# Attention by pairs of heads in a two-model fp32 kernel: scores on TensorE's row halves, values in plain fp32 on its column halves

## The chip, the cores and the metric

The kernel runs on one core of a Trainium2 chip, in one launch. The metric is device time in microseconds (us), the median over several runs. The kernel before takes 2503.48 us (three runs, 2503.0 to 2504.59). Times of single instructions come from one profiled execution and are given in us or ns.

## What is computed

Two small models run one after the other on 256 tokens of width 1024, all in fp32. Each has two layers. The first mixes a convolution, a neighbourhood attention ("na"), a dilated attention ("dil") and a windowed attention with a sink ("swa"), each of the three with 4 heads of 64 dims; the second mixes a Fourier branch, a convolution and a latent attention with 8 heads, over a stream x and, in its first layer, a context stream as well. Every attention comes down to this, for each head:

```python
s = jnp.einsum("bqhd,bkhd->bhqk", q, k) * scale + bias     # 256 x 256 scores of a head
p = jax.nn.softmax(s, axis=-1)
o = jnp.einsum("bhqk,bkhd->bqhd", p, v)                    # 64 dims of values
```

In the second model x looks at x and context (512 keys) and the context at itself (256 keys). The rest of the reference is projections, feed-forward blocks and norms, and these hold nearly all of the work.

## The kernel before

**Products in three parts.** TensorE gets its operands as `float32r`, a reduced fp32 that passes through the array once. To keep fp32's precision each operand is split into a high part and a low part: `parts` (L297 to L299) has ScalarE copy the source into a `float32r` tile and VectorE subtract it from the source. `mm3` (L301 to L305) then makes a product as high x high, high x low and low x high. L303, L304 and L305 are therefore the lines of nearly all matmuls of the profile.

**Weights** stream in from HBM, up to 512 KB a piece, are split by `parts` and used once. Activations stand with dims on the partitions and tokens along the free axis; a product of 256 tokens streams 256 columns, one of both streams together 512.

**Attention of the first model** (`attend1`, L826) is a generator for one head with three stages. Scores: two query tiles of 128, three matmuls each, with 64 rows of the array (`rows` is the upper or lower half, by the head's parity `e`), then bias, maximum, exponential and division on VectorE and ScalarE. Transpose: four 128 x 128 transposes of the probabilities into one PSUM bank (`tp`), then `parts` into PT. Values: `mm3` of V's 128 columns (both heads of the pair, of which one head's 64 are wanted) with PT, for two key tiles, into `py`; the head's 64 rows of `py` go through `parts` into `yt`, and `yt` is what the branch's products read.

**Order of the work.** `mix1` has 12 heads as a pipeline over slots: in a slot head k makes its scores, head k-1 its transposes, head k-2 its values, and after each of the three `more()` (L671) takes a unit from `fill` (projections of gates, of the convolution's input, and the branches' products, whose units read `yt`) and a few taps of the convolution on VectorE. A unit of gates is 24 matmuls of 256 columns. The order in which the instructions of an engine stand in the program is made by the build from this, with some moved between neighbours.

**Attention of the second model** (`attend2`, L1419) is the same for one head of one stream, with `mix2`'s slots around it: scores with all 128 rows, in a PSUM bank for each query tile; transposes, 8 for a head of x, 4 for one of the context; `parts` into PT; `mm3` for four or two key tiles of V, of 128 columns of which 64 are wanted.

In names such as `natp`, `diltp` and `hdtp` the first letters are the phase (na, dil, swa, hd for the second model's heads) and `tp` the PSUM tile, for the transposes and the values alike; `nasc`, `dilsc` and `swasc` are scores, `nar` is PT, `qkvV` and `vr` are V, `trr` and `hdr4b` are the values' results, `g1ps` a gates' product, `b1ps` a branch's, `ident` the identity of a transpose, `ones` a 128 x 128 tile of 1/1024 for sums over partitions. Those sums (L325, L326, L789 and others) are the only plain fp32 matmuls of the kernel; every other one is `float32r` or a transpose.

Of the kernel before, what the change touches and what calls it, by code (L numbers as in the profile page):

```python
# [17 lines left out]
P = 128  # L18
# [12 lines left out]
# ---------------------------------------------------------------- layout on the host  # L31
# [40 lines left out]
def host_arrays(inp):  # L72
# [10 lines left out]
    # [layer, chunk, quarter, 128, 2 row tiles, 512]  # L83
# [76 lines left out]
    # neighbourhood: bias of each pair inside the window, no weight outside  # L160
# [7 lines left out]
    # dilated: in how many of the three groups a key is seen  # L168
# [4 lines left out]
    # as a bias: the logarithm of the count  # L173
# [19 lines left out]
    # the queries' table has the scores' scale in it  # L193
# [15 lines left out]
# ---------------------------------------------------------------- the program  # L209


class Net:
# [13 lines left out]
    # -- tiles  # L226
# [42 lines left out]
    # -- weights  # L269
# [6 lines left out]
    def weights(self, src, raw=None):  # L276
        """High and low parts of a [128, a, b] piece of weights."""
# [29 lines left out]
    # -- rms norm over the partitions of several tiles; gives -2 / sqrt(mean + eps) on every partition  # L307
# [21 lines left out]
    def rsqrt(self, ps, w, f=1.0):  # L329
        """-2 / f / sqrt(f * ps + eps): f as the sums are over 1/1024, not the mean."""  # L330
# [14 lines left out]
    # -- constants  # L345
    def setup(self):
# [12 lines left out]
        # gains carry the -1/2 that norm_fin leaves  # L359
# [34 lines left out]
    def setup_later(self):  # L394
        """What the first model's first products don't need."""
# [28 lines left out]
    def ctx_root(self):  # L424
        """The root of the second stream's first norm."""
# [23 lines left out]
    # -- modulation: silu(c) @ w_mod, each column's sum along the free axis  # L449
# [7 lines left out]
    def mod_step(self, n, upto=(LAYERS,)):  # L457
        """The next n sums, before (layer, step, column), behind the weights split last."""
# [12 lines left out]
    def mod_in(self, l, step):  # L471
        """Per stream: factor on the normed x and shift of a step."""
# [14 lines left out]
    def mod_out(self, l, step):  # L487
        """Per stream: gate of a step."""
# [23 lines left out]
    def add_x(self, st, d, ps, f=1.0):  # L512
        """x += f * ps, and its squares for the next norm."""
# [6 lines left out]
    def gained(self, d):  # L520
        """A row tile of x with its gain but not the root: the first products after a norm don't wait for the root."""
# [10 lines left out]
    def mix1(self, l, R):  # L532
# [7 lines left out]
        def rope_tables():  # L540
            """Rope tables with the gains of the rotated dims."""
# [18 lines left out]
        def headnorm(lo, n, rope):  # L560
            """Head norms: rsqrt of the mean squares, one Newton step on the seed; then the rotation."""
# [23 lines left out]
        def to_heads(i):  # L585
            """Two heads' dims to the partitions."""
# [14 lines left out]
        for c in range(4):  # L601
# [69 lines left out]
        def more():  # L671
            if fill:
                fill.pop(0)()
            if conv:
                with self.tc.issue_after(self.split.ins):
                    next(conv, None)
# [55 lines left out]
    def token_root(self, st):  # L732
        """The root with a token on each partition."""
# [8 lines left out]
    def times(self, src, h, n=T, bank=None):  # L742
        """One column tile of the weights times all row tiles of h."""
# [6 lines left out]
    def conv_in(self, l, h, us):  # L750
        """a * sigmoid(g), twice, with room for the taps; a unit of work for each column tile."""
# [19 lines left out]
    def conv(self, l, us, Y):  # L771
        """31 taps, the two halves of the channels in turn; layer norm, silu."""
# [52 lines left out]

    def attend1(self, l, kind, p, e, qkT, V, yt):  # L826
        """One head: scores and softmax; transpose; values."""
# [3 lines left out]
        hd = (p + 2 * e) if kind == "swa" else (2 * p + e)  # L831
        kp, vp = (k0, v0) if kind == "swa" else (k0 + p, v0 + p * P)
        rows = slice(64 * e, 64 * e + 64)
        self.phase = kind
        ps = self.psc().rearrange("p (a b) -> p a b", a=2)
# [3 lines left out]
        s = self.t("sc1", [P, 512], 3, pool=big).rearrange("p (a b) -> p a b", a=2)  # L839
        if kind == "na":  # L840
            bias = self.t("nab", [P, 2, T], 2, pool=big)
            nc.sync.dma_start(bias, self.a["nab"][l, hd])
        else:
            bias = self.dmask if kind == "dil" else self.smask
        nc.vector.scalar_tensor_tensor(s, ps, 0.125, bias, ALU.mult, ALU.add)
        nm = self.t("nm", [P, 2], 4, pool=big)
        sm = self.t("sm", [P, 2], 4, pool=big)
        nc.vector.tensor_reduce(nm, s, AX.X, ALU.max, negate=True)
        if kind == "swa":
            sk = self.c1(l, "sink", hd)  # L850
            nsk = self.nsink[:, l, hd:hd + 1]
            nc.vector.tensor_tensor(nm, nm, nsk.to_broadcast([P, 2]), ALU.min)
        es = s
        for qt in range(2):
            nc.scalar.activation(es[:, qt, :], s[:, qt, :], AF.Exp, bias=nm[:, qt:qt + 1], accum_out=sm[:, qt:qt + 1])
        if kind == "swa":
            ex = self.t("ex", [P, 2], 2, pool=big)
            nc.scalar.activation(ex, nm, AF.Exp, bias=sk)
            nc.vector.tensor_tensor(sm, sm, ex, ALU.add)
        nc.vector.reciprocal(sm, sm)  # L860
        for qt in range(2):
            nc.scalar.activation(es[:, qt, :], es[:, qt, :], AF.Copy, scale=sm[:, qt:qt + 1])
        yield
        self.phase = kind
        pt = self.ptp().rearrange("p (a b) -> p a b", a=2)
        for kt in range(2):
            for qt in range(2):
                nc.tensor.transpose(pt[:, kt, qt * P:qt * P + P], es[:, qt, kt * P:kt * P + P], self.ident)
        PT = self.r4(2, 2, T)
        self.parts(PT[:, 0], PT[:, 1], pt)  # L870
# [3 lines left out]
        for kt in range(2):  # L874
# [3 lines left out]
        if kind == "swa":  # L878
            dst, tl = slice(64 * (hd % 2), 64 * (hd % 2) + 64), hd // 2
        else:  # L880
            dst, tl = rows, p
        self.parts(yt[dst, tl, 0, :], yt[dst, tl, 1, :], py[rows, :])
        yield

    def gates(self, l, n, h):
        """2 * sigmoid - 1 of the gates of one branch, a unit of work for each column tile."""
# [36 lines left out]
    def ffn1(self, l, R):  # L923
# [64 lines left out]
    # ================================================================ second model  # L988
# [554 lines left out]
```

## Time and profile before

| | |
|---|---|
| median of three runs | 2503.48 us |
| span of the profiled execution, first to last instruction | 2502.6 us |
| TensorE busy | 2482.6 us, 99% |
| VectorE busy | 1853.8 us, 74% |
| ScalarE busy | 1220.6 us, 49% |
| clock granted to TensorE | 0.999 of full speed |

The profile gives no other time for its execution than the span; the median of the runs is 0.9 us longer. A matmul's duration in the trace is its latency, with the pipeline's filling and draining; what a stream of matmuls costs is the distance from one start to the next, which is read from a timeline. A plain fp32 matmul stands as two records, since the hardware makes it from two. VectorE, ScalarE and the DMA queues run beside TensorE.

### The profile page before, as it was taken

The numbers are of one execution on the slowest core, as the hardware profiler recorded it, in microseconds if no ns is written. First come the engines' busy times: TensorE is split into PE (matmuls) and PEld (weight loads), VectorE is DVE, ScalarE is ACT, GpSimd is POOL, SyncE is SP. The second block draws the span as 40 slices with busy tenths as digits, with TensorE's granted clock in tenths as the row PEclk, the third lists the DMA queues.
The fourth block names the chain that finished last, engine by engine and source line by source line (L and its number), as shares of the span: only waits on it lengthen the run. The fifth ranks groups of instructions, "written<-read, shape, count | busy, mean of one in ns | idle before, by whom it ended". The sixth has DMA issues, their size and how long they took to land.

```text
span 2502.6 us, 39819 instructions
## 1 busy us (share of the span) xinstructions
PE 2482.6 (99%) x15339; PEld 2206.8 (88%) x15339; DVE 1853.8 (74%) x3256; ACT 1220.6 (49%) x2132; POOL 1.2 (0%) x14
## 2 busy tenths in 40 slices
PE   8999999999999999999999999999999999999998
PEld 7999999899999988888888888888888888889998
DVE  8888987988998886776758875655765643689655
ACT  7676665766665522223536632222532223567544
POOL 0000000000000000000000000000000000000000
PEclk9999999999999999999999999999999999999999
DMA  7545657555666664664311344544445742333564
GB/s 248 176 139 176 201 178 237 171 160 160 205 214 210 198 208 149 207 181 131 113 59 39 106 152 126 177 143 128 125 145 161 242 151 76 88 115 124 183 205 124
DMA packets 123853, 395.94 MB, mean 158 GB/s; under 512 B 14352, under 2 KB 17168, under 8 KB 123408
## 3 DMA queue, kind: packets, MB, share of 16 engines
q1 hardware_dynamic: 123664, 393.41, 50.4%
q8 instruction: 120, 1.97, 0.3%
q14 instruction: 69, 0.57, 0.1%
HBM read 392.30 MB, written 1.05 MB: 157 GB/s over the span
## 4 chain that ended last, share of the span: by engine, by line
PE 96%; DVE 2%; ACT 1%; DMA 0%; issue 0%; SPq 0%; DVEq 0%; ACTq 0%
PE wops L303 13%; PE wops L304 13%; PE wops L305 13%; PE dnps L305 6%; PE dnps L304 6%; PE dnps L303 6%; PE upps L305 3%; PE upps L303 3%; PE upps L304 3%; PE qkvps L304 1%; PE qkvps L305 1%; PE qkvps L303 1%; PE cvps L303 1%; PE cvps L305 1%; PE cvps L304 1%; PE latps L304 1%
## 5 line engine op out<-in xcount | busy, mean ns | idle before, releaser
L298 ACT CAST wowhi<-woraw 128x1024 fp32r<-128x1024 f32 (+3 forms) x266 | 245.9, 927 | 585.0 <-PE wops L304 362.0
L304 PE MATMUL wops<-wor,wowhi 128*128 128x512 f32 (+2 forms) x1371 | 479.8, 350 | 0.0
L303 PE MATMUL wops<-wor,wowhi 128*128 128x512 f32 (+2 forms) x1371 | 479.6, 350 | 0.0
L305 PE MATMUL wops<-wor,wowlo 128*128 128x512 f32 (+2 forms) x1371 | 479.1, 349 | 0.0
L299 DVE TENSOR_TENSOR wowlo<-woraw,wowhi 128x1024 fp32r<-128x1024 f32 (+3 forms) x266 | 283.9, 1070 | 216.8 <-ACT wowhi L298 208.6
L303 PEld LDWEIGHTS wops<-wor,wowhi 128*128 128x128 f32 x1371 | 257.5, 188 | 38.2 <-PE wops L304 0.2
L304 PEld LDWEIGHTS wops<-wor,wowhi 128*128 128x128 f32 x1371 | 257.8, 188 | 37.4 <-DVE wor L1024 0.2
L305 PEld LDWEIGHTS wops<-wor,wowlo 128*128 128x128 f32 x1371 | 257.8, 188 | 37.1
L298 ACT CAST dnwhi<-dnraw 128x768 fp32r<-128x768 f32 (+2 forms) x144 | 125.1, 870 | 288.1 <-PE dnps L304 180.4
L299 DVE TENSOR_TENSOR dnwlo<-dnraw,dnwhi 128x768 fp32r<-128x768 f32 (+2 forms) x144 | 143.6, 999 | 68.4 <-ACT dnwhi L298 65.9
L305 PE MATMUL upps<-hr,upwlo 128*128 128x256 f32 x656 | 184.1, 282 | 1.5 <-DVE upwlo L299 1.5
L303 PE MATMUL upps<-hr,upwhi 128*128 128x256 f32 x656 | 184.5, 281 | 0.0
L304 PE MATMUL upps<-hr,upwhi 128*128 128x256 f32 x656 | 183.9, 280 | 0.0
L468 DVE SCALAR_TENSOR_TENSOR dnjunk<-dnwm,cond 128x1024 bf16<-128x1024 f32 x134 | 163.4, 1219 | 4.3 <-DMA dnwm<-in_wm 3.2
L305 PE MATMUL dnps<-dnr,dnwlo 128*128 128x512 f32 (+1 forms) x371 | 142.6, 384 | 0.0
L303 PE MATMUL dnps<-dnr,dnwhi 128*128 128x512 f32 (+1 forms) x371 | 142.2, 383 | 0.0
L304 PE MATMUL dnps<-dnr,dnwhi 128*128 128x512 f32 (+1 forms) x371 | 141.5, 381 | 0.0
L468 DVE SCALAR_TENSOR_TENSOR wojunk<-wowm,cond 128x1024 bf16<-128x1024 f32 x114 | 138.8, 1218 | 0.0
L305 PEld LDWEIGHTS upps<-hr,upwlo 128*128 128x128 f32 x656 | 123.1, 188 | 2.2 <-DVE upwlo L299 2.2
L303 PEld LDWEIGHTS upps<-hr,upwhi 128*128 128x128 f32 x656 | 123.9, 189 | 0.0
L304 PEld LDWEIGHTS upps<-hr,upwhi 128*128 128x128 f32 x656 | 123.5, 188 | 0.0
L1109 DVE TENSOR_TENSOR wof<-wof,wops 128x512 f32<-128x512 f32 (+1 forms) x59 | 35.5, 602 | 110.8 <-PE wops L305 110.7
(722 smaller groups left out, 6419.3 us busy)
## 6 DMA issues: line engine op xcount, KB each, us to landing
woraw<-in_w2u SPq DMA_DIRECT2D x132, 512.0 KB, 3.7
upraw<-in_w1u SPq DMA_DIRECT2D x82, 512.0 KB, 4.2
wowm<-in_wm SPq DMA_DIRECT2D x73, 512.0 KB, 4.3
dnwm<-in_wm SPq DMA_DIRECT2D x67, 512.0 KB, 4.0
dnraw<-in_w2u SPq DMA_DIRECT2D x44, 512.0 KB, 3.8
woraw<-in_w2d SPq DMA_DIRECT2D x48, 384.0 KB, 3.1
woraw<-in_w2d SPq DMA_DIRECT2D x48, 320.0 KB, 2.9
qkvraw<-in_w1q SPq DMA_DIRECT2D x24, 512.0 KB, 4.6
```

The source lines that it names most:

```text
L298: act = self.nc.scalar.copy(hi, src)
L299: return act, self.nc.vector.tensor_tensor(lo, src, hi, ALU.subtract)
L303: mm(ps, L[0], R[0], start=st, stop=False)
L304: mm(ps, L[0], R[1], start=False, stop=False)
L305: mm(ps, L[1], R[0], start=False, stop=sp)
L468: nc.vector.scalar_tensor_tensor(junk, self.wm, 1.0, self.cond[:, s, :], ALU.mult, ALU.mult, accum_out=self.M[l][s][step][:, j:j + 1])
L1109: nc.vector.tensor_tensor(s, s, pss[1], ALU.mult)
```

## The change

Heads go by pairs. In `attend1` the six score matmuls of a head and those of its partner are written in turn, one on the upper 64 rows, one on the lower, each head into its own PSUM bank. Softmax follows for the one head and the other; the transposes, 4 for each head, go into two banks, of which ScalarE copies one and VectorE the other into a plain fp32 PT tile: the probabilities are not split any more. V is kept as plain fp32, also without a split. Values are plain fp32 matmuls with 64 columns of weights (`V[kt][:, d]`, one head) and 256 columns streamed: the even head's go to partitions 0 to 63 of `py`, the odd one's to 64 to 127, one after the other for each key tile. Both heads' results leave `py` in one `parts` of 128 partitions (for swa two of 64). In `attend2` scores stay as they are; PT is plain fp32 (ScalarE copies the first query tile, VectorE the second; the context's is copied by ScalarE alone), and the values of a pair are made when its odd head comes to that stage.

`mix1` has 6 pairs in place of 12 heads, so 8 slots in place of 14, and takes 2, 2 and 1 units of fill after the three stages in place of 1, 1 and 1. The scores' buffer has 4 tiles in place of 3. The diff's core (comments that were taken out are left out here):

```diff
-        V = [self.t("V1", [P, 2, 640], 2, F32R, pool=big) for _ in range(2)]
+        V = [self.t("V1", [P, 640], 2, pool=big) for _ in range(2)]
...
-                        hi, lo = [V[tt][:, i, dst:dst + n] for i in range(2)]
-                        nc.scalar.activation(hi, piece, AF.Copy, scale=r)
-                        nc.vector.scalar_tensor_tensor(lo, piece, r, hi, ALU.mult, ALU.subtract)
+                        nc.scalar.activation(V[tt][:, dst:dst + n], piece, AF.Copy, scale=r)
...
-            heads += [self.attend1(l, kind, p, e, qkT, V, tile_) for p in range(2) for e in range(2)]
+            heads += [self.attend1(l, kind, p, qkT, V, tile_) for p in range(2)]
...
         for slot in range(len(heads) + 2):
             work(slot)
-            more()
+            more(2)
             work(slot - 1)
-            more()
+            more(2)
             work(slot - 2)
-            more()
+            more(1)
...
+        pss = [self.psc().rearrange("p (a b) -> p a b", a=2) for _ in range(2)]
         for qt in range(2):
-            s = slice(qt * P, qt * P + P)
-            self.mm3(ps[:, qt, :], [x[rows, s] for x in qkT[q0 + p]], [x[rows, :] for x in qkT[kp]], True, True)
+            c = slice(qt * P, qt * P + P)
+            for i, j, st, sp in ((0, 0, True, False), (0, 1, False, False), (1, 0, False, True)):
+                for e in range(2):
+                    nc.tensor.matmul(pss[e][:, qt, :], qkT[q0 + p][i][rows[e], c], qkT[kp][j][rows[e], :],
+                                     start=st, stop=sp)
...
-        PT = self.r4(2, 2, T)
-        self.parts(PT[:, 0], PT[:, 1], pt)
+        PT = self.t("r4", [P, 1028], 15)[:, :1024].rearrange("p (a b c) -> p a b c", a=2, b=2)
+        for e in range(2):
...
+            if e == 0:
+                nc.scalar.copy(PT[:, e], pt)
+            else:
+                nc.vector.tensor_copy(PT[:, e], pt)
...
-        for kt in range(2):
-            self.mm3(py, (V[kt][:, 0, vp:vp + P], V[kt][:, 1, vp:vp + P]), (PT[:, 0, kt], PT[:, 1, kt]),
-                     kt == 0, kt == 1)
+        self.values(py, [V[kt][:, vp:vp + P] for kt in range(2)], [[PT[:, e, kt] for kt in range(2)] for e in range(2)])
...
+    def values(self, py, V, PT):
+        n = len(V)
+        for kt in range(n):
+            for e in range(2):
+                d = slice(64 * e, 64 * e + 64)
+                self.nc.tensor.matmul(py[d, :], V[kt][:, d], PT[e][kt], start=kt == 0, stop=kt == n - 1)
...
-        for kt in range(nk):
-            v = V[k0 + kt]
-            self.mm3(py, (v[:, 0, c], v[:, 1, c]), (PT[0][:, kt, :], PT[1][:, kt, :]), kt == 0, kt == nk - 1)
-        rows = slice(64 * e, 64 * e + 64)
-        o = slice(s * T, s * T + T)
-        self.parts(att[p][rows, 0, o], att[p][rows, 1, o], py[rows, :])
+        if e:
+            py = self.ptp()[:, :T]
+            c = slice(p * P, p * P + P)
+            self.values(py, [V[k0 + kt][:, c] for kt in range(nk)],
+                        [[PTs[s, h][:, kt, :] for kt in range(nk)] for h in (hd - 1, hd)])
+            o = slice(s * T, s * T + T)
+            self.parts(att[p][:, 0, o], att[p][:, 1, o], py)
```

Three places on TensorE show how the order moves. First the scores of the first heads of the first layer, before (`nasc145` is the head's bank, `cips` the fill):

```order
L591 MATMUL trtp137_662<-ident_64,qkvgt40_202 128x128
L591 MATMUL trtp137_662<-ident_64,qkvgt42_204 128x128
L303 MATMUL nasc145_682<-qkvr448_210,qkvr447_209 128x256
L304 MATMUL nasc145_682<-qkvr448_210,qkvr447_209 128x256
L305 MATMUL nasc145_682<-qkvr448_210,qkvr447_209 128x256
L303 MATMUL nasc145_682<-qkvr448_210,qkvr447_209 128x256
L304 MATMUL nasc145_682<-qkvr448_210,qkvr447_209 128x256
L305 MATMUL nasc145_682<-qkvr448_210,qkvr447_209 128x256
L303 MATMUL cips153_707<-qkvr476_373,ciwhi151_703 128x256
```

and now (`nasc145` and `nasc146` are the banks of the two heads; twelve such rows stand in a row there):

```order
L591 MATMUL trtp137_656<-ident_64,qkvgt42_204 128x128
L841 MATMUL nasc145_676<-qkvr448_210,qkvr447_209 128x256
L841 MATMUL nasc146_677<-qkvr448_210,qkvr447_209 128x256
L841 MATMUL nasc145_676<-qkvr448_210,qkvr447_209 128x256
L841 MATMUL nasc146_677<-qkvr448_210,qkvr447_209 128x256
```

Six matmuls of one head have become twelve of two heads in turn. In the whole program the 144 score matmuls of the first model stood in 26 runs between other work, and stand in 20 now.

Second the values of a head of na, before, between two units of gates:

```order
L305 MATMUL g2ps265_1431<-qkvr4122_584,g2wlo264_1428 128x256
L303 MATMUL natp266_1459<-nar4241_1285,qkvV144_206 128x256
L304 MATMUL natp266_1459<-nar4241_1285,qkvV144_206 128x256
L305 MATMUL natp266_1459<-nar4241_1285,qkvV144_206 128x256
L303 MATMUL natp266_1459<-nar4241_1285,qkvV145_207 128x256
L304 MATMUL natp266_1459<-nar4241_1285,qkvV145_207 128x256
L305 MATMUL natp266_1459<-nar4241_1285,qkvV145_207 128x256
L303 MATMUL g2ps270_1474<-qkvr476_373,g2whi268_1470 128x256
```

and now, of a pair (a row with x2 is the even head's matmul and the odd one's):

```order
L304 MATMUL g2ps245_1277<-qkvr4122_580,g2whi243_1273 128x256
L305 MATMUL g2ps245_1277<-qkvr4122_580,g2wlo244_1274 128x256
L901 MATMUL natp246_1305<-nar4202_1005,qkvV144_206 64x256 x2
L901 MATMUL natp246_1305<-nar4202_1005,qkvV145_207 64x256 x2
L303 MATMUL g2ps250_1318<-qkvr476_371,g2whi248_1314 128x256
L304 MATMUL g2ps250_1318<-qkvr476_371,g2whi248_1314 128x256
L305 MATMUL g2ps250_1318<-qkvr476_371,g2wlo249_1315 128x256
```

Twelve `float32r` matmuls of 128 output rows have become four plain fp32 ones of 64. The program has 384 value matmuls before and 128 now, the latter in 20 runs: 12 of 4, 4 of 8 and 4 of 12.

Third the last values of na and what follows them, now (`trr` is the values' result, `b1ps` the branch's product that reads it; before, 54 other matmuls and 4 transposes stood between):

```order
L901 MATMUL natp279_1530<-nar4234_1223,qkvV145_207 64x256 x2
L303 MATMUL b1ps283_1543<-trr4142_673,b1whi281_1539 128x256
L304 MATMUL b1ps283_1543<-trr4142_673,b1whi281_1539 128x256
L305 MATMUL b1ps283_1543<-trr4142_673,b1wlo282_1540 128x256
L841 MATMUL swasc284_1559<-qkvr452_214,qkvr451_213 128x256
L841 MATMUL swasc285_1560<-qkvr452_214,qkvr451_213 128x256
```

The branch's product now stands right behind the values that it needs.

## Rows read from the trace of the kernel before

**Rows 1.** The page: engines' busy time, clock in 40 slices, chain by engine.

```profile
PE 2482.6 (99%) x15339; PEld 2206.8 (88%) x15339; DVE 1853.8 (74%) x3256; ACT 1220.6 (49%) x2132; POOL 1.2 (0%) x14
PEclk9999999999999999999999999999999999999999
PE 96%; DVE 2%; ACT 1%; DMA 0%; issue 0%; SPq 0%; DVEq 0%; ACTq 0%
```

**Rows 2.** Busy time by stretch: first layer's mix, second model's second attention.

```profile
core 0: us, PE busy (x) PEld busy (x) DVE busy (x) ACT busy (x) POOL busy (x), PEclk, DMA share, GB/s
50.00:245.00 195.00, 194.70 (x1563) 188.23 (x1562) 170.28 (x318) 132.03 (x254) 0.24 (x4) 1.00 0.53 162
...
2225.00:2290.00 65.00, 63.57 (x430) 56.92 (x431) 55.51 (x116) 48.27 (x110) 0.00 (x0) 1.00 0.20 62
```

**Rows 3.** Values' matmuls by tile: min/median/max ns, first and last start.

```profile
L303 PE MATMUL natp<-nar,qkvV x16: 276/280/283, 85.2 to 537.5; 128*128 128x256 f32 x16
L303 PE MATMUL hdtp<-hdwhi,vr x64: 274/281/392, 1337.6 to 2291.2; 128*128 128x256 f32 x64
L303 PE MATMUL hdtp<-hdr,vr x16: 277/283/299, 1339.3 to 1401.9; 128*128 128x256 f32 x16
```

**Rows 4.** Timeline of TensorE, values of a head: start us, duration us, what.

```profile
117.66 0.28 PE L305 MATMUL natp<-nar,qkvV 128*128 128x256 f32 x1
117.77 0.28 PE L303 MATMUL natp<-nar,qkvV 128*128 128x256 f32 x1
117.89 0.28 PE L304 MATMUL natp<-nar,qkvV 128*128 128x256 f32 x1
118.01 0.28 PE L305 MATMUL natp<-nar,qkvV 128*128 128x256 f32 x1
```

**Rows 5.** Timeline of TensorE, plain fp32 sums of the convolution's norm.

```profile
173.25 0.59 PE L789 MATMUL cotp<-cicacc,ones 128*128 128x256 f32 x2
173.68 0.59 PE L790 MATMUL cotp<-cicacc,ones 128*128 128x256 f32 x2
```

**Rows 6.** Timelines of TensorE's loads and matmuls, transposes of a head.

```profile
72.86 0.46 PEld L868 LDWEIGHTS natp<-ident,nasc 128*128 128x128 f32 x4
...
72.96 0.60 PE L868 MATMUL natp<-ident,nasc 128*128 128x128 f32 x4
```

**Rows 7.** Timeline of TensorE, one run of scores among other products.

```profile
130.14 0.28 PE L305 MATMUL g2ps<-qkvr,g2wlo 128*128 128x256 f32 x1
130.35 0.38 PE L303 MATMUL dilsc<-qkvr,qkvr 64*128 64x256 f32 x1
130.57 0.27 PE L304 MATMUL dilsc<-qkvr,qkvr 64*128 64x256 f32 x1
130.68 0.28 PE L305 MATMUL dilsc<-qkvr,qkvr 64*128 64x256 f32 x1
...
131.04 0.27 PE L305 MATMUL dilsc<-qkvr,qkvr 64*128 64x256 f32 x1
131.24 0.38 PE L303 MATMUL b1ps<-trr,b1whi 128*128 128x256 f32 x1
131.46 0.28 PE L304 MATMUL b1ps<-trr,b1whi 128*128 128x256 f32 x1
```

**Rows 8.** Timelines of ScalarE and VectorE behind the values of Rows 4.

```profile
118.95 0.37 ACT L298 CAST trr<-natp 64x256 fp32r<-64x256 f32 x1
...
118.62 0.87 DVE L783 SCALAR_TENSOR_TENSOR cicacc<-cirt,qkvp,cicacc 128x256 f32<-128x256 f32 x2
119.52 0.43 DVE L299 TENSOR_TENSOR trr<-natp,trr 64x256 fp32r<-64x256 f32 x1
```

**Rows 9.** The split of a second-model head's probabilities, by tile.

```profile
L298 ACT CAST hdwhi<-hdtp x32: 567/586/601, 1326.4 to 2288.5; 128x512 fp32r<-128x512 f32 x32
L299 DVE TENSOR_TENSOR hdwlo<-hdtp,hdwhi x32: 664/681/693, 1327.7 to 2289.2; 128x512 fp32r<-128x512 f32 x32
```

**Rows 10.** TensorE's longest wait in the second model's attention: total us, times, longest.

```profile
PE hdsc L303 <- ACT hdQ L298: 0.5, 1, 0.5
```

More of the change, by code (lines that the diff above doesn't have):

```diff
@@ L669, in work, with more @@
                 next(heads[k])
[L671 to L676, printed above, removed]
+        def more(n):
+            for _ in range(n):
+                if fill:
+                    fill.pop(0)()
+                if conv:
+                    with self.tc.issue_after(self.split.ins):
+                        next(conv, None)
         for slot in range(len(heads) + 2):
             work(slot)
-            more()
+            more(2)
             work(slot - 1)
-            more()
+            more(2)
             work(slot - 2)
-            more()
+            more(1)
             if slot == 0:
@@ L830, in attend1 @@
         q0, k0, v0 = {"na": (0, 2, 0), "dil": (4, 6, 256), "swa": (8, 10, 512)}[kind]
-        hd = (p + 2 * e) if kind == "swa" else (2 * p + e)
-        kp, vp = (k0, v0) if kind == "swa" else (k0 + p, v0 + p * P)
-        rows = slice(64 * e, 64 * e + 64)
+        swa = kind == "swa"
+        kp, vp = (k0, v0) if swa else (k0 + p, v0 + p * P)
+        rows = [slice(64 * e, 64 * e + 64) for e in range(2)]
+        hds = [(p + 2 * e) if swa else (2 * p + e) for e in range(2)]
         self.phase = kind
-        ps = self.psc().rearrange("p (a b) -> p a b", a=2)
+        pss = [self.psc().rearrange("p (a b) -> p a b", a=2) for _ in range(2)]
@@ L846, in attend1 @@
[L846 to L862, printed above, removed]
+            c = slice(qt * P, qt * P + P)
[3 more added lines that the diff above has]
+                                     start=st, stop=sp)
@@ new lines, in attend1 @@
+        ess = []
+        for e in range(2):
+            hd, ps = hds[e], pss[e]
+            s = self.t("sc1", [P, 512], 4, pool=big).rearrange("p (a b) -> p a b", a=2)
+            if kind == "na":
+                bias = self.t("nab", [P, 2, T], 2, pool=big)
+                nc.sync.dma_start(bias, self.a["nab"][l, hd])
+            else:
+                bias = self.dmask if kind == "dil" else self.smask
+            nc.vector.scalar_tensor_tensor(s, ps, 0.125, bias, ALU.mult, ALU.add)
+            nm = self.t("nm", [P, 2], 4, pool=big)
+            sm = self.t("sm", [P, 2], 4, pool=big)
+            nc.vector.tensor_reduce(nm, s, AX.X, ALU.max, negate=True)
+            if swa:
+                sk = self.c1(l, "sink", hd)
+                nsk = self.nsink[:, l, hd:hd + 1]
+                nc.vector.tensor_tensor(nm, nm, nsk.to_broadcast([P, 2]), ALU.min)
+            for qt in range(2):
+                nc.scalar.activation(s[:, qt, :], s[:, qt, :], AF.Exp, bias=nm[:, qt:qt + 1], accum_out=sm[:, qt:qt + 1])
+            if swa:
+                ex = self.t("ex", [P, 2], 2, pool=big)
+                nc.scalar.activation(ex, nm, AF.Exp, bias=sk)
+                nc.vector.tensor_tensor(sm, sm, ex, ALU.add)
+            nc.vector.reciprocal(sm, sm)
+            for qt in range(2):
+                nc.scalar.activation(s[:, qt, :], s[:, qt, :], AF.Copy, scale=sm[:, qt:qt + 1])
+            ess.append(s)
@@ L863, in attend1 @@
         yield
         self.phase = kind
-        pt = self.ptp().rearrange("p (a b) -> p a b", a=2)
-        for kt in range(2):
-            for qt in range(2):
-                nc.tensor.transpose(pt[:, kt, qt * P:qt * P + P], es[:, qt, kt * P:kt * P + P], self.ident)
-        PT = self.r4(2, 2, T)
-        self.parts(PT[:, 0], PT[:, 1], pt)
+        PT = self.t("r4", [P, 1028], 15)[:, :1024].rearrange("p (a b c) -> p a b c", a=2, b=2)
+        for e in range(2):
+            pt = self.ptp().rearrange("p (a b) -> p a b", a=2)
+            for kt in range(2):
+                for qt in range(2):
+                    nc.tensor.transpose(pt[:, kt, qt * P:qt * P + P], ess[e][:, qt, kt * P:kt * P + P], self.ident)
+            if e == 0:
+                nc.scalar.copy(PT[:, e], pt)
+            else:
+                nc.vector.tensor_copy(PT[:, e], pt)
@@ L873, in attend1 @@
         py = self.ptp()[:, :T]
-        for kt in range(2):
-            self.mm3(py, (V[kt][:, 0, vp:vp + P], V[kt][:, 1, vp:vp + P]), (PT[:, 0, kt], PT[:, 1, kt]),
-                     kt == 0, kt == 1)
-        if kind == "swa":
-            dst, tl = slice(64 * (hd % 2), 64 * (hd % 2) + 64), hd // 2
-        else:
-            dst, tl = rows, p
-        self.parts(yt[dst, tl, 0, :], yt[dst, tl, 1, :], py[rows, :])
+        self.values(py, [V[kt][:, vp:vp + P] for kt in range(2)], [[PT[:, e, kt] for kt in range(2)] for e in range(2)])
+        if swa:
+            dst = slice(64 * p, 64 * p + 64)
+            for e in range(2):
+                self.parts(yt[dst, e, 0, :], yt[dst, e, 1, :], py[rows[e], :])
+        else:
+            self.parts(yt[:, p, 0, :], yt[:, p, 1, :], py)
         yield
+    def values(self, py, V, PT):
+        n = len(V)
+        for kt in range(n):
+            for e in range(2):
+                d = slice(64 * e, 64 * e + 64)
+                self.nc.tensor.matmul(py[d, :], V[kt][:, d], PT[e][kt], start=kt == 0, stop=kt == n - 1)
     def gates(self, l, n, h):
@@ L1329, in fill @@
                 self.gated_add(s, d, ps[:, s * T:s * T + T])
-        gx = [self.attend2(0, h, Q, K, V, att) for h in range(8)]
-        gc = [self.attend2(1, h, Q, K, V, att) for h in range(8)] if qs == 2 else []
+        gx = [self.attend2(0, h, Q, K, V, att, PTs) for h in range(8)]
+        gc = [self.attend2(1, h, Q, K, V, att, PTs) for h in range(8)] if qs == 2 else []
         def step(g, k):
@@ L1455, in attend2 @@
         if s == 0:
-            PT = [self.t(n, [P, 1024], 4, F32R).rearrange("p (a b) -> p a b", a=4) for n in ("whi", "wlo")]
+            PT = self.t("wlo" if e else "whi", [P, 1024], 4).rearrange("p (a b) -> p a b", a=4)
             for qt in range(2):
@@ L1460, in attend2 @@
                     nc.tensor.transpose(pt[:, kt, :], es[qt][:, kt * P:kt * P + P], self.ident)
-                self.parts(PT[0][:, :, qt * P:qt * P + P], PT[1][:, :, qt * P:qt * P + P], pt)
-        else:
-            x = self.r4(2, 2, 256)
-            PT = [x[:, 0], x[:, 1]]
+                if qt == 0:
+                    nc.scalar.copy(PT[:, :, qt * P:qt * P + P], pt)
+                else:
+                    nc.vector.tensor_copy(PT[:, :, qt * P:qt * P + P], pt)
+        else:
+            if e == 0:
+                PTs["c"] = self.t("r4", [P, 1028], 15)[:, :1024].rearrange("p (a b c) -> p a b c", a=2, b=2)
+            PT = PTs["c"][:, e]
             pt = self.ptp().rearrange("p (a b) -> p a b", a=2)
@@ L1468, in attend2 @@
                     nc.tensor.transpose(pt[:, kt, qt * P:qt * P + P], es[qt][:, kt * P:kt * P + P], self.ident)
[L1469 removed]
+            nc.scalar.copy(PT, pt)
+        PTs[s, hd] = PT
         yield
[L1471 to L1478 removed]
+        if e:
[5 more added lines that the diff above has]
+            self.parts(att[p][:, 0, o], att[p][:, 1, o], py)
         yield
```

20 lines of the change are left out of this document (5 added, 15 removed).

## The prediction

> **What bounds the kernel now.** I read the page first: TensorE is busy for 2482.6 of 2502.6 us at full clock in every slice, and 96% of the chain that ended last is its own instructions [rows 1]. So I look at the attention stretches, where something else could end last: VectorE is busy for 170 of 195 us in the first layer's mix and for 56 of 65 us in the last attention, close but below TensorE's 195 and 64 [rows 2], and the longest wait on another engine in the second model's attention is 0.5 us [rows 10]. TensorE is therefore the bound there too, and the change is worth what it does to TensorE's stream of instructions. What one costs is the distance from start to start, not the 0.28 us of its record: for a float32r matmul of 256 columns 0.35 us for three, 0.118 each with the decimals of many [rows 4].
>
> **Part 1, the values.** Removed: 384 matmuls, nine groups of 16 for the first model, 3 x 64 and 3 x 16 for the second [rows 3]: 384 x 0.118 = 45.3 us. Added: 128 plain fp32 matmuls of 256 columns. The only plain fp32 matmuls of the trace are sums with a full 128 x 128 tile: the two start 0.43 us apart, each two records of 0.215 [rows 5]. So alone, one costs 3.6 of the old ones. All depends on whether the even and the odd head, on different column halves, run at the same time; nothing in this trace uses column halves. The bounds: one after the other, 128 x 0.43 = 55.0 us, a loss of 9.7. Side by side, 64 x 0.43 = 27.5 us, and since the odd head's second record can only begin when its first is through, each of the 20 runs has about 0.215 us at its end with one half idle, 4.3 us: 31.8 us, a gain of 13.5. I take side by side: the two halves share neither output rows nor weights, and the four weight loads of a pair, even at the full width's 0.107 us each [rows 6], fill 0.43 us and no more, and they are half as wide.
>
> The trace shows a weight load and the matmul before it overlapping in the full array: a load of 128 columns takes 0.107 us in a series of them [rows 6], and matmuls that each have one still start 0.118 us apart [rows 4], with loads busy 88% and matmuls 99% of the span [rows 1]. The Trainium skill ("TensorE: Matmul & The Clock Gate", Part 3, "What overlaps and what doesn't") says that a load overlaps running matmuls only when the row group differs; by that, column halves, which use all rows alike, would wait for every load, and the values would come near the first bound. The trace disagrees for full rows, so I give the rule no weight of its own beyond the serial case below.
>
> **Part 2, the scores.** 144 matmuls in either kernel, at 0.118 us: 17.0 us before. Now neighbours use different row halves and banks. If halves run side by side and their loads too, 72 x 0.118 = 8.5 us plus about 0.3 us where a run has an odd count: a gain of 8.2. If loads queue up, a load is the pace: the transposes, with one load of 128 columns for each 128 streamed, load every 0.107 us (0.46 less 0.14 for the last, over three) and start every 0.109 us [rows 6]; 144 x 0.109 = 15.7, a gain of 1.3. If nothing overlaps, 0. I take 1.3: the transposes' row is the only one where loads are the pace, and no row shows two loads at once.
>
> **Part 3, changing from full rows to half.** A run of scores has a price at its ends: from the last full matmul at 130.14 to the second one after the run at 131.46 there are 1.32 us for eight matmuls that at 0.118 make 0.94 [rows 7], so 0.38 us, at all four starts around the two changes. 26 runs x 0.38 = 9.9 us before; 20 runs x 0.38 = 7.6 now. New are 20 runs on column halves, whose ends no row shows. Their bounds: 0.38 as above, and half of it, 0.19, if the half-wide load is what stands exposed; below that there is no reason, as the array changes its shape in the same way. I take 0.33, nearer to the row that shows a change: 6.6 us. Sum of this part: 7.6 + 6.6 - 9.9 = 4.3 us lost.
>
> **Part 4, waits.** Behind na's last values the branch's product now stands directly. After the values of rows 4 the results were there late: the last matmul starts at 118.01, the high part is done at 119.32, the low part at 119.95 [rows 4, 8], since ScalarE finishes an activation first and VectorE's convolution taps are ahead in its queue. The new order puts three ready matmuls, nine scores in two runs and their changes in between, some 2 us, so the wait is 0 to 1 us for a layer: 0.5 in all. On the other side, V, PT and half of the results' splits leave ScalarE and VectorE: in the last attention alone 16 instructions of 0.68 us on VectorE and 16 of 0.59 on ScalarE, half of the 32 of each, become 8 copies on each [rows 9]. Both engines are off the path, so this is worth only the waits that it shortens, of which the longest is 0.5 us [rows 10]; I count nothing. If the cover got thin instead, TensorE has less of its own work between a softmax and its use, but VectorE and ScalarE lose more work than TensorE does. Fewer slots of `mix1` leave no unit of fill behind: 40 units were taken in 42 calls, and are now in 40. DMAs stay the same and none is on the chain.
>
> **Sum.** -13.5 - 1.3 + 4.3 + 0.5 = -10.0 us against the span of 2502.6: 2492.6; the median lies 0.9 us above the span, so 2493.5 us.
>
> **The rivals.**
> - Row halves overlap fully, loads too: -13.5 - 8.2 + 4.3 + 0.5 = -16.9, 2486.6 us. For it: the scores' operands come from different partitions, and their banks differ. Against it: no row has two loads at once. The Trainium skill ("TensorEngine Tiling (Array Packing)", Tiling Modes, Key Properties) says that tiles are independent and that different ones load and multiply in parallel; by that it would be this case, and no run yet shows it.
> - Column halves don't overlap, and the kernel is **slower**: plain fp32 then costs 55.0 us for 45.3. With scores at 0.109 us +9.7 - 1.3 + 4.3 + 0.5 = +13.2, 2516.7 us; with scores fully overlapped +6.3, 2509.8 us. It decides from the point where a pair's key tile costs over 0.59 us (0.43 side by side, 0.86 in series): the values may cost 45.3 + 1.3 - 4.3 - 0.5 - 4.3 (run ends with one half idle) = 37.5 us, over 64. For it: a plain fp32 matmul is several passes with two sets of weights, and two streams of columns read the same partitions at the same time, where float32r's 0.118 us for 256 columns is already longer than half of the 0.215 of a two-pass record [rows 4, 5], as if reading were near a limit. [...]
> - Columns overlap in part, at some 0.59 us a pair and key tile: no change, 2503.5 us.
>
> **How the numbers follow.** Chances: the forecast 0.34, rows overlapped too 0.24, partial 0.08, series with rows overlapped 0.12, series with rows at the loads' pace 0.16, something else (new waits, or less than expected of them) 0.06. The range takes in the first four, from the second's 2486.6 less 3.6 for ends of runs at 0.19 and waits gone, to 2513, above the 2509.8; left out is most of the worst case and little else, about 0.19: 2483 to 2513. A measurement of this kernel can tell about 0.2%, 5 us, from no change. Faster by more: the first two less the forecast's tail of dear run ends, 0.56. Slower by more: the two serial cases less a tenth, plus a share of the rest, 0.27. Within: 0.17.
>
> **What would show it.** In the trace of the changed kernel a pair's four value records (two of each head) with the odd head's first starting within some ns of the even head's second, and 0.43 us from key tile to key tile, would show side by side; 0.86 us series. Scores: starts 0.109 us apart, or 0.059 on average if loads overlap. Run ends: 0.38 us around scores as before, 0.19 to 0.38 around values. The product behind na's last values: its fourth matmul late by under 1 us. TensorE should stay above 98% busy; if it falls to VectorE's or ScalarE's pace in either attention, Part 4 is wrong, and if the records of a pair's values stand in series, Part 1 is, and with it the sign.

## The result: 2477.1 us, faster by 1.05%

The changed kernel takes 2477.1 us (2476.9 to 2478.3), the kernel before in the same comparison 2504.0 (2503.0 to 2504.6): a ratio of 0.9895, 95% interval 0.9881 to 0.9909. The forecast was 2493.5, its range 2483 to 2513: the sign was right, the size too small by 16 us, and the time lies below the range. The profiled execution spans 2475.1 us where the one before spans 2502.6, so 27.5 us have gone.

The page of the changed kernel, the rows that answer to [rows 1]:

```profile
span 2475.1 us, 39396 instructions
...
PE 2456.9 (99%) x15211; PEld 2170.2 (88%) x15211; DVE 1812.9 (73%) x3180; ACT 1197.4 (48%) x2084; POOL 1.2 (0%) x14
...
PE 95%; DVE 2%; ACT 1%; DMA 0%; issue 0%; SPq 0%; DVEq 0%; ACTq 0%
```

TensorE still is the bound, at 99% busy and 95% of the chain that ended last. So the question is what each product costs in its stream, as it was in the prediction. TensorE's timeline for values of the second model (start us, duration us, what; a bracket at a row's end, where there is one, holds the idle time before it and what ended it), which answers to [rows 4]:

```profile
2232.45 0.27 PE L305 MATMUL waps<-cvr,wawm 128*128 128x256 f32 x1
2232.74 0.43 PE L901 MATMUL hdtp<-hdwhi,vr 128*64 128x256 f32 x1
2232.75 0.43 PE L901 MATMUL hdtp<-hdwlo,vr 128*64 128x256 f32 x1
2233.01 0.38 PE L901 MATMUL hdtp<-hdwhi,vr 128*64 128x256 f32 x1
2233.02 0.38 PE L901 MATMUL hdtp<-hdwlo,vr 128*64 128x256 f32 x1
2233.22 0.38 PE L901 MATMUL hdtp<-hdwhi,vr 128*64 128x256 f32 x1
2233.23 0.38 PE L901 MATMUL hdtp<-hdwlo,vr 128*64 128x256 f32 x1
```

`hdwhi` holds the even head's probabilities and `hdwlo` the odd's. Each plain fp32 product is two records, each with a weight load of its own (the profile's page counts as many loads as matmuls). The two heads' records start 6 to 7 ns apart (0.01 us here); the next two follow 0.27 us behind the first two of a run, and from then on every two start 0.216 us behind the two before. So the column halves run side by side in full, and the loads of both are hidden. The timelines for a run of scores, which answers to [rows 7], and for the values of a first-model pair:

```profile
90.70 0.28 PE L305 MATMUL g1ps<-qkvr,g1wlo 128*128 128x256 f32 x1
90.91 0.97 PE L841 MATMUL dilsc<-qkvr,qkvr 64*128 64x256 f32 x12
91.81 0.39 PE L303 MATMUL g1ps<-qkvr,g1whi 128*128 128x256 f32 x1
92.03 0.28 PE L304 MATMUL g1ps<-qkvr,g1whi 128*128 128x256 f32 x1
...
104.16 1.08 PE L901 MATMUL natp<-nar,qkvV 128*64 128x256 f32 x8
105.17 0.39 PE L303 MATMUL g2ps<-qkvr,g2whi 128*128 128x256 f32 x1
```

Twelve scores take 0.90 us from the first start to the next full-width product, where six took 0.89 before (130.35 to 131.24 in [rows 7]). Inside the run, by the trace, the starts stand 3 or 4 ns and then some 114 ns apart (218 behind the first two): two products, each with its own weight load, for 0.118 us.

Where the 27.5 us come from, summed from the starts of TensorE's products in the two traces (a run of halves is counted with what it costs at its two ends, as in the prediction's Part 3):

| | before, us | after, us | difference |
|---|---|---|---|
| scores: 26 runs, now 20 | 27.0 | 17.3 | -9.7 |
| values: 384 products, now 128 in 20 runs | 46.2 | 34.8 | -11.4 |
| products that the change doesn't touch: `upps`, `wops`, `qkvps`, `cvps` (0.8 of the difference a wait at `cvps`) | 1396.5 | 1392.2 | -4.3 |
| all else of TensorE's time, waits among it | | | -2.1 |

### The profile page after: what moved, and what is told of

It reads as the page before. It is cut to its first block, busy times and chain, and to the rows that moved or that the text cites. A ratio compares the mean times of both kernels' runs of the same rounds, so it can differ in the third digit from the quotient of the medians.

```text
span 2475.1 us, 39396 instructions
## 1 busy us (share of the span) xinstructions
PE 2456.9 (99%) x15211; PEld 2170.2 (88%) x15211; DVE 1812.9 (73%) x3180; ACT 1197.4 (48%) x2084; POOL 1.2 (0%) x14
## 3 DMA queue, kind: packets, MB, share of 16 engines
HBM read 392.30 MB, written 1.05 MB: 159 GB/s over the span
## 4 chain that ended last, share of the span: by engine, by line
PE 95%; DVE 2%; ACT 1%; DMA 0%; issue 0%; SPq 0%; DVEq 0%; ACTq 0%
PE wops L305 13%; PE wops L303 13%; PE wops L304 13%; PE dnps L304 6%; PE dnps L305 6%; PE dnps L303 6%; PE upps L305 3%; PE upps L303 3%; PE upps L304 3%; PE qkvps L304 1%; PE qkvps L305 1%; PE qkvps L303 1%; PE cvps L303 1%; PE cvps L305 1%; PE cvps L304 1%; PE latps L304 1%
```

## The experiments

My theory after the two traces: (a) row halves run side by side, loads too; (b) column halves run side by side; (c) both because neighbours in the order are of different halves; (d) what is left is a price at the ends of each run, and waits. The rivals stand with each run. The changed kernel is the measure; it took 2477.1 us in the comparison above and 2477.7 beside the later runs.

**Scores head by head.** The order is undone, nothing else.

```
+for e in range(2):
 for qt in range(2):
...
     for i, j, st, sp in ((0, 0, True, False), (0, 1, False, False), (1, 0, False, True)):
-        for e in range(2):
```

> The changed kernel, but a pair's twelve score products stand head by head (six of the even head's row half, then six of the odd's) and no longer alternate. Theory (products of the two row halves run side by side, loads included, and TensorE starts its products in the order in which they stand): 72 products that lay beside a partner need their own 0.118 us again, save the one at each run's middle, so about +8 us on the changed kernel, about 2485 us, ratio to before about 0.993; the gaps between the starts in a run read 0.118 each and one of a few ns. Rival 1 (the gain on scores is not from the order, but from waits and from fewer mode changes): within 1 us of the changed kernel, 2477, ratio 0.9895. Rival 2 (only the running overlaps, so that the loads set the pace, as the prediction took it): +1 to +3 us.

Measured: 2480.2 us (2479.6 to 2480.4), ratio 0.9904 [0.9890, 0.9919]: 2.5 to 3.1 us above the changed kernel, not the 8 that I expected. By the number alone that is the second rival. The trace says otherwise: the same run of twelve takes 1.24 us where it took 0.90,

```profile
90.75 1.31 PE L841 MATMUL dilsc<-qkvr,qkvr 64*128 64x256 f32 x12
91.99 0.39 PE L303 MATMUL g1ps<-qkvr,g1whi 128*128 128x256 f32 x1
```

and its starts, by the trace, stand 222, 118, 7, 113, 110, 5, 109, 10, 106, 117 and 120 ns apart: two products alone, then mostly twins, then three alone. A pace set by loads would show even steps. In the program the run is six products of the even head and then six of the odd's, with nothing between; the first twin starts with the even head's third and, by its record of 0.38 us, as only the first product on a half has it, is the odd head's first, four places further on. All 20 runs take 21.0 us for 17.3, so +3.7 on TensorE. Part (c) of my theory was wrong in its strict form: a product need not be the next in the order, TensorE started one that stood four places further back, ahead of the three between.

**Values head by head.**

```
-for kt in range(n):
-    for e in range(2):
+for e in range(2):
+    for kt in range(n):
```

> The changed kernel, but the value products of a pair stand head by head: all key tiles on the even head's column half, then all on the odd's. Theory (the column halves run side by side only where neighbours in the order are of different halves): 128 records of 0.21 us come out from beside their partners, less about one per run of each pair, +20 to +27 us on the changed kernel, 2497 to 2504, ratio 0.9975 to 1.0005. This is also the price of the case 'column halves one after the other' of the prediction. Rival (the chip finds the partner by itself, or the two records of one product already overlap): within 2 us of 2477.

Measured: 2485.1 us (2484.6 to 2485.9), ratio 0.9926 [0.9909, 0.9942]: +7.4 to +8.0, neither the theory's 20 to 27 nor the rival's 2 at most. The second model's runs, with four products of the even head ahead of four of the odd's, show why:

```profile
1328.59 1.29 PE L901 MATMUL hdtp<-hdwhi,vr 128*64 128x256 f32 x5
1329.51 0.43 PE L901 MATMUL hdtp<-hdwlo,vr 128*64 128x256 f32 x1
1329.72 0.38 PE L901 MATMUL hdtp<-hdwhi,vr 128*64 128x256 f32 x1
1329.78 0.38 PE L901 MATMUL hdtp<-hdwlo,vr 128*64 128x256 f32 x1
...
1331.13 1.19 PE L901 MATMUL hdtp<-hdr,vr 128*64 128x256 f32 x5
```

Five of the even head's eight records have started when the odd head's first does (the x5 of the first row; by the trace it starts 6 ns behind the fifth), ahead of the even head's sixth: again four places, counted in records, which are two to a product here. In the first model a head has two products, four records, so that the odd head's first record starts with the even head's first, 13 ns apart, and those 12 runs lose nothing (1.21 us each, as in the changed kernel). All runs take 42.15 us for 34.76, +7.4. The Trainium skill ("TensorE: Matmul & The Clock Gate", Part 3, "What overlaps and what doesn't") says that products start and end strictly in the order of the program; for products on different halves these rows disagree, since a record of the odd head started while three earlier ones of the even head had not.

**Values in plain fp32, without column halves.**

```
-self.nc.tensor.matmul(py[d, :], V[kt][:, d], PT[e][kt], start=kt == 0, stop=kt == n - 1)
+self.nc.tensor.matmul(py[:, e * T:e * T + T], V[kt], PT[e][kt], start=kt == 0, stop=kt == n - 1)
```

The two loops change places as well, so that a head's products stand together, and the results of the two heads, now in two halves of a bank, leave it in a split for each head.

> The changed kernel, but the value products are plain fp32 on all 128 columns of TensorE, with each head's result in its own half of a PSUM bank and half of it read; no column halves and so none of their 20 mode changes. Theory: 128 products of 2 records of 0.215 us are 55.0 us where the column halves took 34.8 with their mode changes: +20 us on the changed kernel, about 2497, ratio about 0.9975. Against the run with the values head by head it says what a mode change costs: 20 x 0.355 = 7.1 us less the overlaps left there (about 24 x 0.2 = 4.8). Rival (full-width plain fp32 is as quick as the column halves): 2477 to 2479.

Measured: 2502.0 us (2501.4 to 2505.3), ratio 0.9994 [0.9985, 1.0003]: +24 to +25. The prediction's serial price, 55.0 us, less the column runs' 34.8 makes +20.2 of it, and the records do stand 0.216 us apart here, one after the other. Some 4 to 5 us are left. The traced execution took 2505.3 us, 3.3 above the median, so it holds more than the median does. What TensorE waited for in it (us in total, times, longest):

```profile
PE qkvtp L325 <- DVE qkvS L316: 2.7, 1, 2.7
PE b1ps L303 <- ACT trr L298: 2.0, 2, 1.0
```

The changed kernel shows 0.3 at the first and nothing at the second. The second is this form's own: it comes back in the next run, and Part 4 below has its rows. The first differs from trace to trace (1.2 and 1.9 for the instructions of the kernel before, 0.3 and 0.4 for the changed kernel's), so how much of it the median has is not shown. Without column halves the change brings 1.7 us, the scores included, and its interval holds no change.

**Scores by pairs alone, values as before.**

```
-V = [self.t("V1", [P, 640], 2, pool=big) for _ in range(2)]
+V = [self.t("V1", [P, 2, 640], 2, F32R, pool=big) for _ in range(2)]
...
-self.values(py, [V[kt][:, vp:vp + P] for kt in range(2)], [[PT[:, e, kt] for kt in range(2)] for e in range(2)])
+for e in range(2):
+    for kt in range(2):
+        self.mm3(py[:, e * T:e * T + T], (V[kt][:, 0, vp:vp + P], V[kt][:, 1, vp:vp + P]),
+                 (PTs[e][:, 0, kt], PTs[e][:, 1, kt]), kt == 0, kt == 1)
```

The second model's values go back to the old form in the same way, head by head, and each head's results leave in a split of their own.

> Only one part of the change: scores by pairs on the row halves as in the changed kernel; values again in three float32r parts on all columns with V and the probabilities split, in both models (the two heads of a first-model pair one after the other). Theory (scores bring -9.7 us with their mode changes, values -10.5, the rest is waits): 10.5 us above the changed kernel and up to 3 more for the splits' waits, 2487 to 2491, ratio 0.9935 to 0.995. Rival (scores bring what the prediction took, -3.6, and the values or waits the rest): 2499 to 2501, ratio 0.9985. Rival (nearly all of it is scores): 2478 to 2482.

Measured: 2493.6 us (2492.2 to 2495.3), ratio 0.9959 [0.9944, 0.9974]: 10.1 below the kernel before, 16 above the changed one. So neither rival holds: the scores, with the order by pairs that goes with them, bring about ten without the new values. They stand in 14 runs here and not in 20, which take 14.4 us without the wait behind two of them, so -12.6 on 27.0. That the time still lies 2.6 above the range that I expected has its row: the product behind na's last values, whose results are split for each head apart in this form, waits for ScalarE in both layers, 3.0 us in all, as in the run above.

```profile
126.30 0.39 PE L303 MATMUL b1ps<-trr,b1whi 128*128 128x256 f32 x1 [1.39 <-ACT trr L298]
```

So this run has a wait that neither the kernel before nor the changed one has, and the 16 us between it and the changed kernel are not the values' alone.

**The changed kernel again.** No edit.

> The changed kernel once more, word for word, beside the next three on the same chip. Of the 27.5 us between the two profiles' spans, about 4 lie in stretches that the change does not touch (the first model's up projection 244.2 against 242.7 us for the same 2016 products, the output products 992.4 against 991.1 for the same 5461). Theory (a property of the kernel's layout, the same in each execution): 2477 us, and the same two sums to 0.2 us. Rival (chance of one execution): the median stays but the two sums fall back toward 244.2 and 992.4.

Measured: 2477.7 us (2477.0 to 2478.0), ratio 0.9894 [0.9879, 0.9909]; `upps` 242.9 us, the output products 991.0. The quicker pace of untouched products repeats: it belongs to the program, not to one execution.

**Other places in memory for the kernel before.**

```
-s = self.t("sc1", [P, 512], 3, pool=big)...
+s = self.t("sc1", [P, 512], 4, pool=big)...
```

> The kernel before with one buffer more for the score tiles and nothing else: every instruction stays, and the tiles behind it in SBUF lie 2 KB further. Theory (the pace of products that the change does not touch hangs on where their operands lie): the up projection's sum moves by 0.5 us or more from 244.2, the time by 0.5 to 4 us either way. Rival (places play no part; the pace went with the work that the change takes off the other engines): 2503.5 within 1 us, the up projection's sum 244.2 within 0.2.

Measured: 2503.5 us (2502.5 to 2505.4), ratio 1.000 [0.9991, 1.0009]; `upps` 244.3, the output products 992.1. This shift does nothing, so the rival's first half, that places play no part, holds as far as one shift can tell; that the pace went with the work taken off the other engines is not shown. The wait of 0.8 us at `cvps` is not in this trace, whose instructions are those of the kernel before, so that it is missing in the changed kernel need not be the change's doing. Over the programs run here the same 2016 products of `upps` took from 241.9 to 244.3 us; what sets that stays open.

**Values right behind scores.** A pair's values move up behind the next pair's scores, to save changes between full rows and halves.

```
 work(slot)
-more(2)
+work(slot - 2)
+more(3)
 work(slot - 1)
 more(2)
-work(slot - 2)
-more(1)
```

> The changed kernel with another order in the first model's mixing: in each slot a pair's values stand right behind the next pair's scores, so that 8 of the 20 runs of column halves follow a run of row halves with no full-width product between, and the scores stand in 16 runs where they stood in 20. Theory 1 (each change of form costs by itself; a direct change from row halves to column halves costs one change, about 0.2 us, where there were two): 4 runs x 0.44 and 8 x 0.2 us, -3.4 us on the changed kernel, 2473.6. Theory 2 (the price is paid only towards and from full-width products, the direct change is free): -1.8 - 8 x 0.4 = -5 us, 2472. Rival (the products that now stand elsewhere wait for the vector and scalar engines, since values are nearer to their probabilities): no gain, 2477, or up to 2 us more.

Measured: 2475.5 us (2474.9 to 2476.9) beside the changed kernel's 2477.0 to 2478.0, ratio to before 0.9886 [0.9872, 0.9901]: 2.2 us less, between theory 1's 3.4 and the rival's nothing, so the rows have to decide. The timeline at one of the eight direct changes:

```profile
107.89 0.28 PE L305 MATMUL g2ps<-qkvr,g2wlo 128*128 128x256 f32 x1
108.09 0.97 PE L840 MATMUL dilsc<-qkvr,qkvr 64*128 64x256 f32 x12
109.00 1.08 PE L900 MATMUL natp<-nar,qkvV 128*64 128x256 f32 x8
110.01 0.39 PE L303 MATMUL g2ps<-qkvr,g2whi 128*128 128x256 f32 x1
```

The run of scores takes 0.91 us here too, so leaving the row halves is paid for as it is towards full rows (0.205 us from the last score to the first value, by the trace, for 0.118 inside a run); what is saved is one change of the two. That is theory 1's mechanism. The scores and the products next to these runs, `b1ps`, `g2ps` and `g3ps`, sum to 3.1 us less; 1.0 went back at `upps` and 0.5 at `qkvps`, which the reorder doesn't touch. (The traced execution took 2476.9 us, 1.5 above the median, so its sums don't tell where all of the 2.2 come from.)

**The same with the scores' runs in one piece.** The last three turns of keys and queries come one slot later.

```
-if slot == 0:
+if slot == 1:
     for i in (8, 10, 9):
         to_heads(i)
```

> As the run with scores next to values, and besides the last three transposes of keys and queries to the heads' layout stand one slot later, so that they no longer cut the second pair's scores: 13 runs of scores (20 in the changed kernel), 6 direct changes from row to column halves. Theory 1 (a change costs 0.44 us a run): 7 x 0.44 + 6 x 0.2 = -4.3 us on the changed kernel, 2472.7. Theory 2 (direct change free): -3.1 - 6 x 0.4 = -5.5, 2471.5. Rival (the later transposes make the sliding-window scores wait, or the earlier values wait): 2475 to 2479.

Measured: 2476.3 us (2476.0 to 2476.7), ratio 0.9889 [0.9872, 0.9905]: below the changed kernel, not below the run before. The scores lose 0.4 us more, but `g1ps`, among which the turns now stand, takes 1.2 more than in the changed kernel. That is the rival's way: the first of the turns waits 0.3 us for VectorE in either layer, by the trace; the order before this step has the lowest median of those run here.

## Why the prediction was too cautious

**The bound** was read right: TensorE, 99% busy in both.

**Part 2, the scores,** is the largest miss. The step that failed is the choice between the ends: the loads as the pace, -1.3 us, taken from the transposes' row [rows 6]. Inside the runs the products went from 17.0 to 8.5 us, the other end. The transposes all load the same full array, so their row shows what one place for weights costs when it is used again and again, and not what two do; I noted that no row shows two loads at once, and should have put the value nearer to the middle. With the runs' ends, the scores bring -9.7, where Parts 2 and 3 together had -3.6. This was the first rival, at 0.24: its mechanism is shown by the starts and by the run head by head, and the run with scores by pairs and the old values shows its size, -10.1 us on the time. The Trainium skill's statement that tiles load and multiply in parallel ("TensorEngine Tiling (Array Packing)", Tiling Modes, Key Properties) stood by that rival, and the starts of the scores agree with it.

**Part 1, the values.** Side by side was right, and 64 x 0.43 = 27.5 us for the pairs is what the trace has, to 0.1. Wrong is the term of 4.3 us for the half-idle end of each run, of which the rows show nothing: the order that TensorE takes is even, odd, even, odd, each head's first record beside the other's first, not the odd head's first beside the even's second. The signature that I gave for it ("the odd head's first starting within some ns of the even head's second") is not what the rows show. And the values before took 46.2 us, not 45.3: by the trace 0.8 of it lies behind the first products of nine runs, whose second ones came 0.02 to 0.19 us late.

**Part 3, the ends of the runs.** Forecast 0.38 us for a run of scores and 0.33 for one of values. Measured are 0.39 for a whole run of scores, 0.44 over all 20, because 12 of them are pieces that other products cut, and each of the 8 odd pieces leaves a score without a twin, and 0.355 for values: 8.8 + 7.1 where I had 7.6 + 6.6. This part held, 1.7 us too low.

**Part 4, waits.** The wait of 0 to 1 us for a layer behind na's last values does not occur: its fourth product starts on time (the fifth, which needs the low part too, some 0.1 us late, by the trace).

```profile
122.51 0.39 PE L303 MATMUL b1ps<-trr,b1whi 128*128 128x256 f32 x1
122.73 0.28 PE L304 MATMUL b1ps<-trr,b1whi 128*128 128x256 f32 x1
122.84 0.28 PE L305 MATMUL b1ps<-trr,b1wlo 128*128 128x256 f32 x1
123.06 0.51 PE L841 MATMUL swasc<-qkvr,qkvr 64*128 64x256 f32 x4
123.49 0.38 PE L303 MATMUL b1ps<-trr,b1whi 128*128 128x256 f32 x1
```

It does occur in both runs that split the results for each head, 2.0 and 3.0 us, and ScalarE's rows show why. The changed kernel, and the odd head's copy in the full-width run:

```profile
122.81 0.36 ACT L298 CAST trr<-natp 128x256 fp32r<-128x256 f32 x1
125.30 0.37 ACT L298 CAST trr<-natp 64x256 fp32r<-64x256 f32 x1 [1.31 <-DVE trr L299]
```

Copied at once, a pair's high part is there at 123.17, 0.32 us ahead of the product that needs it. Split for each head, the odd head's copy stands still for 1.31 us until VectorE has subtracted for the even head, behind its other work. So the margin was thin, and one split for a pair is what kept it. I counted nothing for work taken off ScalarE and VectorE; the last attention's products lose 1.7 us more than their own count explains (4.5 us less until the output products begin, 2.8 by the values), and three gaps that stood there before, 0.40 to 0.64 us by the starts, are gone, though one wait is new. It is the changed kernel's longest in this stretch, 1.0 us (us in total, times, longest):

```profile
PE hdps L303 <- ACT hdwhi L298: 1.0, 1, 1.0
```

So the term that I put at nothing, since both engines are off the path, came to up to 1.7 in this attention; that all of it is the work taken off the two is not shown, for the order changed too. (The longest wait that I read there was 0.5; the view of that stretch has 0.8 at `cvps` ahead of it.)

**Together:** -10.0 by the prediction; -6.1 more by the scores with their ends, -3.6 by the values with theirs, -0.5 by the wait: -20.2. The rest of the 27.5 us are 0.9 that the old values took above their count, 4.3 in products that the change doesn't touch, and 2.1 not told apart. Of the 4.3, the 0.8 at `cvps` need not be the change's, as the run with other places shows; 2.7 is the quicker pace of `upps` and the output products, which repeats and whose cause stays open. The slower rival, column halves one after the other, is refuted by the rows, and its price for the values is borne out: in the full-width run, where they don't run side by side, their 55.0 us against 46.2 and the new waits take back nearly all that the scores bring.

**The range.** Its lower end was the first rival less 3.6 us. It had the rows overlapping, but still with the half-idle ends; with those taken out it would have reached 2478.7, still 1.6 above the time.

## What to carry to other kernels

Where products use half of TensorE's rows or half of its columns, pair two that use different halves, and expect each pair at the price of one: streaming 256 columns, two float32r products on 64 rows each took 0.118 us together, and two plain fp32 products on 64 columns each 0.43. They need not alternate strictly, but in these runs no partner was found more than four records back. A whole run of halves between full products cost about 0.35 to 0.4 us for its two ends, so gather the runs, and put one kind of half right behind the other.

## What the runs showed of the chip that I had not expected

- A product whose half was free started while up to three records ahead of it in the order had not, both for float32r (one record to a product) and for plain fp32 (two): the odd head's first ran beside the even head's third of six, and beside its fifth of eight.
- A direct change from row halves to column halves costs what a change to full rows does at that place, 0.205 us from start to start for 0.118, and saves the second change.
- The same 2016 products at the same granted clock (0.999) took 241.9 to 244.3 us in one program or another, and 242.7 and 242.9 in two executions of one.
- With a split for each head behind na's last values, ScalarE's copy of the second head waited 1.3 to 2.3 us for VectorE's subtraction of the first.
